# Another start for stationary weight parts, and sums of weight blocks at other steps

## The chip, the cores and the metric

The kernel runs on one core of one Trainium2 chip. Its metric is the device time of one execution in microseconds (us), the median of the runs.

## The reference

One hybrid layer over 256 tokens of width 1024, batch 1, all in float32:

```
h = rmsnorm(x) * (1 + scale) + shift          # shift, scale, gate = c @ w_ada + b_ada
qa ka va za qm km vm zm om ig fg ga gm = split(h @ w_in)     # w_in: 1024 x 11272
ya = (causal attention(qa, ka, va; 8 heads) * silu(za)) @ w_att_proj
hm = chunkwise mLSTM(silu(conv(qm, km)), vm, gates ig, fg; 4 heads)
ym = (rmsnorm(sigmoid(om) * hm) * silu(zm)) @ w_ml_proj
out = x + gate * ((sigmoid(ga) * ya + sigmoid(gm) * ym) @ w_out)
```

## The kernel before

**Products from split parts.** Each float32 operand of a large product is split into a rounded high part and the rest: h into hTh and hTl, a weight tile into wh (ScalarE, a copy, L502) and wl (VectorE, or GpSimd, named POOL, for some tiles, L506). A product is then three: high by high, low by high, high by low.

**Two orientations.** A chunk of 512 output columns is made in four groups, each with a pair of 128-row blocks of the contraction. Chunks of kind "tok" (va, zm, vm, out) have tokens on the output's partitions: the activation is stationary (128x128, loaded into the array), and the weight part streams (L1152 to L1154; for out L1145, and L1172 to L1174 at the end). Chunks of kind "ws" (za, qm, km, att, ga, gm, ml) are made transposed: a 128x128 piece of wh or wl is stationary, and 256 columns of an activation stream (L1159, L1161, L1162): hTh and hTl in za, qm, km, ga and gm, yah and yal in att, ymh and yml in ml. A group has 24 such products. The chunk om is made by seven products of half size, from sums of blocks (L1135 to L1137).

**Buffers.** wh and wl lie in two rings of five buffers of RING floats. WS_AT says how many floats into its buffer a part of a "ws" chunk begins; a part of another chunk begins at its start. Groups are numbered g in the order of place; split(g + 4) is issued at step g, four groups ahead of its products. Weight tiles (raw, six buffers of 1 MB) are loaded by the queue of SyncE (SP) as tiles come free. The output's activations yh and yl begin 16 and 48 floats into their slots (L851).

**Order.** Everything is issued in the order of the program, with no scheduler. Steps beside the main products are hooked to a step number g by at(g, function), and run there, in the order in which they were added, before the products of g. The gates' chain is such a row of steps: gates_0 to gates_5 work on the tile G on ScalarE, VectorE and POOL, gates_4 clears GE on POOL (L611), gates_5 writes GE (L619) and sends G's row to DRAM, gates_T transposes GE on TensorE (L641), gates_6 and gates_7 fetch and mask NM, gates_D takes its exponential.

**The sums.** Four sums of blocks of w_in (two halves each, om_sums in DRAM) are formed by DMAs that POOL issues: om_sum copies a block there (L770) or has a DMA add a block to it (L768). OM_SUMS lists them as (sum, source, add); a whole number as source is another sum. They are read as weight tiles for om later on.

Of the kernel before, what the change touches and what calls it, by code (L numbers as in the profile page):

```python
# [21 lines left out]
NEG = -1e30  # L22
BUCKETS = 32

RING, WS_AT = 1152, 96

COL = dict(qa=0, ka=1024, va=2048, za=3072, qm=4096, km=5120, vm=6144, zm=7168, om=8192,
           ig=9216, fg=9220, ga=9224, gm=10248)
# [21 lines left out]
NV = 344  # L50
OM_PRODUCTS = (((0, 0), 0), (1, 1), ((1, 0), 0), (2, 1), (0, 2), (3, 3), ((1, 1), 2))
OM_FIRST = (0, 1, 4, 5)
OM_SUMS = ((0, (0, 0), False), (2, (0, 1), False), (0, (0, 1), True), (2, (1, 1), True),
           (1, 0, False), (1, (1, 1), True), (3, 1, False), (3, (1, 0), True))
OM_SUM_AT = (5, 8, 11, 14, 20, 26, 32, 38)
W_PIECES = ((0, 512), (512, NR), (512, 1024), (1024, NR))


# [13 lines left out]
def tile_hybrid(ctx: ExitStack, tc: tile.TileContext, x, c, params2, w_row, w_va, ada_mod, ada_gate,  # L72
# [62 lines left out]
    adat, wrow, wsp, hf = {}, {}, {}, {}  # L135
# [235 lines left out]
    def start(name, half=0):  # L371
        return G0[C[name, half]]
# [138 lines left out]
    def at(step, fn, *a):  # L511
        hooks.setdefault(step, []).append((fn, a))
# [528 lines left out]
    at(start("gm") + 1, gate_read)  # L1041
    for q in range(4):
        at(start("ml") + 3 + q, gate_columns, q)
    for (i, src, add), step in zip(OM_SUMS, OM_SUM_AT):
        for hf in range(2):
            at(step + 3 * hf, om_sum, i, src, add, hf)
    T["A"] = {}
    for kh in range(2):
        at(start("qm", 1) + 1 + 4 * kh, h_full, kh)
# [179 lines left out]
```

## Time and profile before

| | |
|---|---|
| three runs | 355.93, 356.88, 356.96 us; median 356.88 |
| the profiled execution | 356.49 us, of which the span from the first to the last instruction is 354.6 |
| granted TensorE clock | 1.000 |
| DMA | 89.33 MB, mean 252 GB/s |
| the sums' queue (software_dynamic) | 8.39 MB, 10.3% of 16 engines' span |

PE is TensorE's products, PEld its weight loads, DVE VectorE, ACT ScalarE, POOL GpSimd, SP SyncE. Rows of groups give line, engine, operation, output<-inputs, shapes and count. "[1.10 <-ACT GE L619]" means that the engine was idle for 1.10 us before this, and what ended that. Starts of products are in us from the span's start; durations include the array's latency, so that products overlap: the pace is seen in the starts.

### The profile page before, as it was taken

Reading aid. Unit: us, or ns where it says so; the run is one execution under the profiler, and the core shown is the slowest. Engines: PE = TensorE matmul, PEld = TensorE weight load, DVE = VectorE, ACT = ScalarE, POOL = GpSimd, SP = SyncE. Lnnn points to the kernel's source line nnn. Section 1 sums busy time; section 2 is a strip of 40 time slices with the busy share of each in tenths; the row PEclk is TensorE's granted clock in tenths of the full one; section 3 lists DMA queues with packets and bytes.
Section 4 is the critical chain, followed back from the end, with each engine's and each line's share of the span. In section 5 each row is a group of like instructions: output and inputs, shape, how many; then the busy total and the mean of one; then the engine's idle time right before and its main releaser. Section 6 shows DMA issues by size and latency. Waiting matters only on the chain.

```text
span 354.6 us, 6241 instructions
## 1 busy us (share of the span) xinstructions
PE 348.4 (98%) x2420; PEld 327.1 (92%) x2420; DVE 262.8 (74%) x393; ACT 221.8 (63%) x344; POOL 100.9 (28%) x97
## 2 busy tenths in 40 slices
PE   8999999999999999999999999999999999999995
PEld 7787889999989999999998888888989999999995
DVE  5999987967973779865868665777777466689842
ACT  4868889799757857675636565677573463655410
POOL 4700004954501665665206242000002121302000
PEclk9999999999999999999999999999999999999999
DMA  7999999997997699395997916677999027363011
GB/s 303 417 415 414 416 418 405 262 365 208 240 298 242 211 357 344 103 352 203 262 355 239 368 81 224 214 273 266 150 262 387 6 86 299 151 206 152 2 61 59
DMA packets 29069, 89.33 MB, mean 252 GB/s; under 512 B 3368, under 2 KB 5296, under 8 KB 28336
## 3 DMA queue, kind: packets, MB, share of 16 engines
q1 hardware_dynamic: 26008, 80.02, 62.4%
q0 software_dynamic: 2880, 8.39, 10.3%
q10 hardware_dynamic: 152, 0.53, 0.4%
q8 instruction: 19, 0.31, 0.3%
q14 instruction: 10, 0.08, 0.1%
HBM read 87.68 MB, written 9.64 MB: 274 GB/s over the span
## 4 chain that ended last, share of the span: by engine, by line
PE 87%; DMA 4%; ACT 4%; DVE 3%; issue 0%; SPq 0%; ACTq 0%
PE mm L1162 13%; PE mm L1161 13%; PE mm L1159 13%; PE pm L203 12%; PE mm L1152 5%; PE mm L1153 5%; PE mm L1154 5%; PE mm L1145 3%; DMA raw<-in_w_in_dram 3%; PE aux L1135 2%; PE aux L1136 2%; PE aux L1137 2%; DVE wl L506 1%; DMA xt<-in_x_dram 1%; ACT wh L502 1%; PE xps L268 1%
## 5 line engine op out<-in xcount | busy, mean ns | idle before, releaser
L506 DVE TENSOR_TENSOR wl<-raw,wh 128x1024 fp32r<-128x1024 f32 (+1 forms) x98 | 121.2, 1253 | 55.1 <-ACT wh L502 54.4
L502 ACT CAST wh<-raw 128x1024 fp32r<-128x1024 f32 (+1 forms) x106 | 106.2, 1015 | 42.9 <-PE mm L1154 16.7
L1159 PE MATMUL mm<-hTh,wh 128*128 128x256 f32 x320 | 91.4, 286 | 0.0
L1162 PE MATMUL mm<-hTh,wl 128*128 128x256 f32 x320 | 90.2, 282 | 0.0
L1161 PE MATMUL mm<-hTl,wh 128*128 128x256 f32 x320 | 90.1, 282 | 0.0
L1159 PEld LDWEIGHTS mm<-hTh,wh 128*128 128x128 f32 x320 | 60.3, 189 | 0.2
L1161 PEld LDWEIGHTS mm<-hTl,wh 128*128 128x128 f32 x320 | 60.3, 188 | 0.2
L1162 PEld LDWEIGHTS mm<-hTh,wl 128*128 128x128 f32 x320 | 60.3, 188 | 0.0
L1152 PE MATMUL mm<-wh,hTh 128*128 128x512 f32 (+1 forms) x112 | 40.5, 362 | 0.0
L1153 PE MATMUL mm<-wl,hTh 128*128 128x512 f32 (+1 forms) x112 | 40.2, 359 | 0.0
L1154 PE MATMUL mm<-wh,hTl 128*128 128x512 f32 (+1 forms) x112 | 40.1, 358 | 0.0
L506 POOL TENSOR_TENSOR wl<-raw,wh 128x1024 fp32r<-128x1024 f32 x8 | 20.9, 2620 | 14.1 <-ACT wh L502 14.1
L1154 PEld LDWEIGHTS mm<-wh,hTl 128*128 128x128 f32 x112 | 21.0, 188 | 2.5
L1152 PEld LDWEIGHTS mm<-wh,hTh 128*128 128x128 f32 x112 | 21.0, 188 | 2.4
L1153 PEld LDWEIGHTS mm<-wl,hTh 128*128 128x128 f32 x112 | 21.1, 188 | 2.3
L188 ACT CAST wrh<-raw 128x512 fp32r<-128x512 f32 (+1 forms) x24 | 18.2, 762 | 7.4 <-DMA raw<-in_w_row_dram 7.4
L193 DVE TENSOR_TENSOR wrl<-raw,wrh 128x512 fp32r<-128x512 f32 (+1 forms) x26 | 20.5, 813 | 0.9 <-ACT wrh L188 0.9
L203 PE MATMUL pm<-wrh,hTh 128*128 128x512 f32 x64 | 19.9, 392 | 0.0
L203 PE MATMUL pm<-wrh,hTl 128*128 128x512 f32 x64 | 19.8, 390 | 0.0
L842 POOL TENSOR_TENSOR attT<-attT,gat 128x1024 f32<-128x1024 f32 x2 | 5.2, 2625 | 50.9 <-ACT gat L841 50.9
L203 PE MATMUL pm<-wrl,hTh 128*128 128x512 f32 x64 | 19.1, 395 | 0.0
L1162 PE MATMUL mm<-yah,wl 128*128 128x256 f32 x64 | 18.0, 281 | 0.0
(244 smaller groups left out, 753.2 us busy)
## 6 DMA issues: line engine op xcount, KB each, us to landing
raw<-in_w_in_dram SPq DMA_DIRECT2D x31, 1024.0 KB, 7.8
adat<-in_ada_mod_dram SPq DMA_DIRECT2D x16, 512.0 KB, 8.8
om_sum<-in_w_in_dram POOLq DMA_DIRECT2D x12, 512.0 KB, 9.6
raw<-in_w_va_dram SPq DMA_DIRECT2D x6, 688.0 KB, 8.9
raw<-in_ada_gate_dram SPq DMA_DIRECT2D x4, 1024.0 KB, 8.2
raw<-in_w_att_proj_dram SPq DMA_DIRECT2D x4, 1024.0 KB, 4.8
raw<-om_sum SPq DMA_DIRECT2D x8, 512.0 KB, 5.6
raw<-in_w_ml_proj_dram SPq DMA_DIRECT2D x4, 1024.0 KB, 5.8
```

The lines of the kernel that those rows point to most:

```text
L188: copy(wsp[k][0][:, c0:c1], wrow[k][:, c0:c1])
L193: e.tensor_tensor(l[:, cs], wrow[k][:, cs], h[:, cs].bitcast(F32), op=OP.subtract)
L203: nc.tensor.matmul(pm[ch][:, t], a[:, k, t * 128:(t + 1) * 128], b[:, cs], start=k == 0 and i == 0, stop=k == KT - 1 and i == 2)
L502: nc.scalar.copy(h, w)
L506: e.tensor_tensor(l, w, h.bitcast(F32), op=OP.subtract)
L1145: nc.tensor.matmul(mmt[ci][:, t, cs], a, w[:, kk, cs], start=first and i == 0 and c0 == 0 and w is wh, stop=last and i == 1 and c0 > 0, sk ...
L1152: nc.tensor.matmul(o, a, wh[:, kk], start=first, stop=False)
L1153: nc.tensor.matmul(o, a, wl[:, kk], start=False, stop=False)
L1154: nc.tensor.matmul(o, b, wh[:, kk], start=False, stop=last)
L1159: nc.tensor.matmul(o, wh[:, kk, cs], sh_[:, k], start=first and i % 2 == 0, stop=False, skip_group_check=True)
L1161: nc.tensor.matmul(o, wh[:, kk, cs], sl_[:, k], start=False, stop=False, skip_group_check=True)
L1162: nc.tensor.matmul(o, wl[:, kk, cs], sh_[:, k], start=False, stop=last and i % 2 == 1, skip_group_check=True)
```

## The change

It moves the start of stationary weight parts in their ring buffers from 96 to 80 floats (384 to 320 bytes). And it gives each sum its own step, with the second half two steps behind the first instead of three, in a slightly other order: the four adds to sums 0 and 2, which stood at steps 11 to 17, now stand at 18, 20, 26 and 28, behind the gates' steps 12 to 17.

```diff
-RING, WS_AT = 1152, 96
+RING, WS_AT = 1152, 80
...
-OM_SUMS = ((0, (0, 0), False), (2, (0, 1), False), (0, (0, 1), True), (2, (1, 1), True),
-           (1, 0, False), (1, (1, 1), True), (3, 1, False), (3, (1, 0), True))
-OM_SUM_AT = (5, 8, 11, 14, 20, 26, 32, 38)
+OM_SUMS = (((0, (0, 0), False), 5), ((2, (0, 1), False), 9), ((0, (0, 1), True), 18), ((1, 0, False), 24),
+           ((2, (1, 1), True), 26), ((1, (1, 1), True), 30), ((3, 1, False), 37), ((3, (1, 0), True), 41))
...
-    for (i, src, add), step in zip(OM_SUMS, OM_SUM_AT):
+    for (i, src, add), step in OM_SUMS:
         for hf in range(2):
-            at(step + 3 * hf, om_sum, i, src, add, hf)
+            at(step + 2 * hf, om_sum, i, src, add, hf)
```

## The prediction

> **What bounds the kernel now.** I read the page from the top: busy times, the clock row, the chain that ended last.
>
> ```profile
> PE 348.4 (98%) x2420; PEld 327.1 (92%) x2420; DVE 262.8 (74%) x393; ACT 221.8 (63%) x344; POOL 100.9 (28%) x97
> PEclk9999999999999999999999999999999999999999
> PE 87%; DMA 4%; ACT 4%; DVE 3%; issue 0%; SPq 0%; ACTq 0%
> ```
>
> TensorE runs 348.4 of 354.6 us at full granted clock and carries 87% of the chain. The time can only fall in two ways: TensorE's products follow each other faster, or its few idle moments go. The change has one part for each. For the pace I asked for the lines that multiply with a stationary weight part (L1159; L1161 and L1162 have the same counts) and for the tail of the output product (L1172), where the roles are exchanged: there the weights stream and yh is stationary.
>
> ```profile
> L1159 PEld LDWEIGHTS mm<-hTh,wh x320: 187/188/193, 82.9 to 305.8; 128*128 128x128 f32 x160
> L1159 PE MATMUL mm<-hTh,wh x320: 279/281/367, 83.0 to 305.9; 128*128 128x256 f32 x160
> L1159 PE MATMUL mm<-yah,wh x64: 279/281/285, 164.2 to 186.6; 128*128 128x256 f32 x64
> L1159 PE MATMUL mm<-ymh,wh x64: 279/281/285, 306.3 to 328.7; 128*128 128x256 f32 x64
> L1172 PEld LDWEIGHTS mm<-wh,yh x32: 187/188/188, 339.9 to 350.4; 128*128 128x128 f32 x32
> L1172 PE MATMUL mm<-wh,yh x32: 276/276/276, 340.0 to 350.5; 128*128 128x256 f32 x32
> ```
>
> Columns are minimum, median and maximum in ns. Both kinds stream 256 columns against a 128x128 stationary block of the same type, and the weight load takes 188 ns in both. Yet the product takes 276 ns without exception at L1172, and 279 to 285 with a stationary weight part. The busy table by stretch gives the pace (a window of length W that overlaps n products of length d has a pace of (W+d)/n):
>
> ```profile
> core 0: us, PE busy (x) PEld busy (x) DVE busy (x) ACT busy (x) POOL busy (x), PEclk, DMA share, GB/s
> 130.00:186.00 56.00, 56.00 (x474) 56.00 (x473) 43.54 (x71) 34.39 (x46) 26.51 (x16) 1.00 0.81 269
> 286.00:290.00 4.00, 4.00 (x36) 4.00 (x36) 1.97 (x4) 3.30 (x12) 1.25 (x1) 1.00 0.00 0
> 308.00:328.60 20.60, 20.60 (x176) 20.60 (x175) 17.58 (x18) 11.36 (x13) 4.58 (x3) 1.00 0.43 154
> 330.00:339.60 9.60, 9.60 (x87) 9.60 (x86) 7.77 (x9) 5.25 (x6) 0.00 (x0) 1.00 0.01 2
> 341.00:350.00 9.00, 9.00 (x82) 9.00 (x81) 3.92 (x8) 0.00 (x0) 0.00 (x0) 1.00 0.24 89
> ```
>
> The first three rows hold products with a stationary weight part: 56.281/474 = 118.7 ns, 4.281/36 = 118.9, 20.881/176 = 118.6. The last two hold the output product: 9.876/87 = 113.5 and 9.276/82 = 113.1. It is not other traffic: 118.9 stands in a row with no DMA at all, 118.7 in one at 269 GB/s. What differs is where the operands lie. In the built program hTh and hTl start 256 bytes past a multiple of 512; yah, yal, ymh, yml and the rings of wh and wl at a multiple of 512; yh 64 and yl 192 bytes past one. With every inner step a multiple of 512, the distance from the streamed to the stationary operand, modulo 512, is 128 for hTh and hTl and 384 for the four others (118.7 ns both), and 64 or 192 in the output product (113.3 ns).
>
> The second part concerns the one place where TensorE waits in mid-kernel:
>
> ```profile
> 105.31 0.27 PE L685 MATMUL aux<-ident,P 128*128 128x128 f32 x1
> 106.68 0.31 PE L641 MATMUL aux<-ident,GE 36*128 36x36 f32 x2 [1.10 <-ACT GE L619]
> ...
> 103.29 1.05 ACT L502 CAST wh<-raw 128x1024 fp32r<-128x1024 f32 x1 [2.12 <-DMA raw<-in_w_in_dram]
> 104.37 1.23 DVE L506 TENSOR_TENSOR wl<-raw,wh 128x1024 fp32r<-128x1024 f32 x1 [1.29 <-ACT wh L502]
> 105.71 0.41 DVE L618 TENSOR_TENSOR G<-G 4x256 f32<-4x256 f32 x1
> 106.21 0.41 ACT L619 ACTIVATE GE<-G 4x256 f32<-4x256 f32 x1 [0.62 <-DVE st L676]
> ```
>
> The transposes of GE (L641) wait 1.10 us for ScalarE's GE, that for VectorE's L618, which stands behind a wl, that behind a cast, and the cast waited 2.12 us for a weight load.
>
> **The change part by part.** *Offset.* No instruction is added or removed; every wh and wl of kind "ws" moves 64 bytes down in the same buffers. The distances become 64 (hTh, hTl) and 320 (the rest). 320+64+64 products on each of three lines are 1344. Nothing in the trace shows a weight part at 320. Bounds: if the distance is what counts, 64 is that of yh, so 113.3, a gain of 5.4 ns x 1344 = 7.3 us; the other end is the slowest steady pace of such products in the trace, in the ga stage (24 from 243.44 to 246.32, 120.0 ns):
>
> ```profile
> 243.44 0.29 PE L1159 MATMUL mm<-hTh,wh 128*128 128x256 f32 x1
> 246.32 0.40 PE L1135 MATMUL aux<-wh,hsum 128*128 128x512 f32 x1
> ```
>
> That would lose 1.3 x 1344 = 1.7 us. I take the end at 113.3, since 960 of the 1344 get exactly yh's distance and the tail is steady there for 192 products. I deduct 0.5 us: some 22 stretches begin behind other products, and I let the first five of each keep the old pace (22 x 5 x 5 ns).
>
> The Trainium skill, page "TensorE: Matmul & The Clock Gate", section "Step-by-step: what each phase is for", says that TensorE reads SBUF through two independent ports, one for the streamed operand and one for weight loads, so that loading the next weights takes nothing from the running product. By that rule this part would bring nothing and the sum would be that of the second rival below. Its weight loads agree (188 ns in both kinds); its products do not (276 against 279 to 285), though no row here shows that the offset is the cause.
>
> *Sums.* Sixteen DMAs of POOL form sums of weight blocks in DRAM (L770 copies, L768 adds into the destination). Only POOL's order changes. At the gates (om_sum_565/566 are the halves of sum 0, 569/570 of sum 2), before:
>
> ```order
> L589 TENSOR_SCALAR G<-G 4x256
> L770 DMA om_sum_566<-in_w_in_dram 256x1x512
> L770 DMA om_sum_569<-in_w_in_dram 256x1x512
> L770 DMA om_sum_570<-in_w_in_dram 256x1x512
> L768 DMA om_sum_565<-in_w_in_dram 256x1x512
> L598 TENSOR_TENSOR G<-G 4x256
> L600 TENSOR_TENSOR G<-G 4x256
> L768 DMA om_sum_566<-in_w_in_dram 256x1x512
> L768 DMA om_sum_569<-in_w_in_dram 256x1x512
> L611 MEMSET GE 36x256
> L768 DMA om_sum_570<-in_w_in_dram 256x1x512
> L704 TENSOR_TENSOR yal<-yf,yah 128x512
> ```
>
> and after, on the same engine (line numbers are one lower):
>
> ```order
> L588 TENSOR_SCALAR G<-G 4x256
> L769 DMA om_sum_569<-in_w_in_dram 256x1x512
> L769 DMA om_sum_570<-in_w_in_dram 256x1x512
> L597 TENSOR_TENSOR G<-G 4x256
> L599 TENSOR_TENSOR G<-G 4x256
> L610 MEMSET GE 36x256
> L703 TENSOR_TENSOR yal<-yf,yah 128x512
> L767 DMA om_sum_565<-in_w_in_dram 256x1x512
> L631 COPY NM<-NM 128x4x128
> ```
>
> All four adds leave the gates' stretch; one copy moves ahead of G's clearing. POOL's own issue time was never in the way:
>
> ```profile
> 75.01 0.88 POOL L586 TENSOR_SCALAR G<-G 4x256 f32<-4x256 f32 x1 [3.72 <-ACT G L584]
> ...
> 91.31 1.71 POOL L768 DMA_DIRECT2D om_sum<-in_w_in_dram  x2
> 93.06 0.31 POOL L611 MEMSET GE<- 36x256 f32 x1
> 97.98 0.41 DVE L612 TENSOR_TENSOR GE<-G 4x256 f32<-4x256 f32 x1
> ```
>
> The copy that moves ahead issues within the 3.72 us that POOL then waits for ScalarE, and GE is cleared at 93.4 and first written at 97.98. What the adds hold up is the DMA engines. Queues from 87 to 92.4 us, then from 92.4 to 103.3, then the page's median landing of all such loads:
>
> ```profile
> q0 software_dynamic: 256, 0.50, 69.5%
> ...
> q0 software_dynamic: 570, 1.11, 59.5%
> raw<-in_w_in_dram SPq DMA_DIRECT2D x3, 1024.0 KB, 14.2
> ...
> raw<-in_w_in_dram SPq DMA_DIRECT2D x31, 1024.0 KB, 7.8
> ```
>
> POOL's queue took 60 to 70% of the engines' time while weight loads took 14.2 us instead of 7.8. The load behind the late cast was issued at 92.47:
>
> ```profile
> 92.47 10.74 DMA raw<-in_w_in_dram
> ```
>
> At 7.8 us it lands at 100.3, before ScalarE is free for the cast (103.29-2.12 = 101.17). Then VectorE's 1.29 us go and GE comes 1.29 us earlier. TensorE, with 144 faster products behind it (0.8 us), would still be there first, so wait and products together give 1.3 us here; without the faster pace it is the 1.1 us of the wait. Next late is VectorE itself, which has no gap left there.
>
> The adds run later, between weight parts of POOL. Before (567/568 are the halves of sum 1):
>
> ```order
> L506 TENSOR_TENSOR wl<-raw,wh 128x1024
> L770 DMA om_sum_568<-om_sum_566 16x8192
> L506 TENSOR_TENSOR wl<-raw,wh 128x1024
> L768 DMA om_sum_567<-in_w_in_dram 256x1x512
> L506 TENSOR_TENSOR wl<-raw,wh 128x1024 x2
> L768 DMA om_sum_568<-in_w_in_dram 256x1x512
> ```
>
> and after:
>
> ```order
> L505 TENSOR_TENSOR wl<-raw,wh 128x1024 x2
> L769 DMA om_sum_567<-om_sum_565 16x8192
> L769 DMA om_sum_568<-om_sum_566 16x8192
> L767 DMA om_sum_569<-in_w_in_dram 256x1x512
> L505 TENSOR_TENSOR wl<-raw,wh 128x1024 x2
> L767 DMA om_sum_570<-in_w_in_dram 256x1x512
> L767 DMA om_sum_567<-in_w_in_dram 256x1x512
> ```
>
> Behind them on POOL wait wl parts, and TensorE for those. Loads that take 14.2 instead of 7.8 us delay a cast by up to 6.4 us; the split runs four steps ahead of the products (4 x 24 x 118.7 ns = 11.4 us), which covers that. I cost it at nothing; uncovered, an add would cost a microsecond or two. No gates' chain lies there.
>
> *Sum.* The profiled execution took 356.49 us. (1344-144) x 5.4 ns = 6.5, less 0.5, plus 1.3 is 7.3: 349.2. The median of the runs, 356.88, stands 0.4 higher, so 349.6.
>
> **Rivals.** *Part of the products only.* Distance 320 appears nowhere before; if yah, yal, ymh and yml keep 118.7, 384 x 5.4 = 2.1 us are missing: 351.7. Also, the pace has a memory. The va products at the same distance ran 12.716/83 = 153.2 ns each before the first transposes, and 157.8 behind them (23 in 3.63 us):
>
> ```profile
> 55.30:67.70 12.40, 12.40 (x83) 12.40 (x82) 11.13 (x13) 10.29 (x15) 8.91 (x7) 1.00 0.97 299
> 71.94 0.32 PE L1153 MATMUL mm<-wl,hTh 128*128 128x344 f32 x1
> 75.57 0.38 PE L658 MATMUL aux<-kT,qT 128*128 128x256 f32 x1
> ```
>
> If stretches behind transposes stay slow, it ends nearer 355.
>
> *No change of pace.* The distance may not be the cause: at L902 to L904, where SD lies 192 bytes from what streams, nine products take 1.08 us, 120 ns each.
>
> ```profile
> 268.94 0.28 PE L902 MATMUL aux<-vaug,SD 128*128 128x258 f32 x1
> 270.02 0.28 PE L1159 MATMUL mm<-hTh,wh 128*128 128x256 f32 x1
> ```
>
> Against it: two thirds of these stream 258 columns, and nine may be too few to settle. Then only the wait goes: 356.88-1.1 = 355.8.
>
> *Slower.* Distance 64 or 320 makes a worse rhythm in L1159 to L1162. It decides from (1.1+1.07)/1344 = 1.6 ns more per product, 120.3. At 120.0 the time is 357.5; with another 5.4 ns per product it is 363.1. Against it: 64 is good wherever the trace has it.
>
> **How the numbers follow.** Faster pace everywhere 0.42 (349.6, own range 348 to 351); part of the products 0.24 (351 to 355.3); no change of pace 0.18 (355.8); slower pace 0.16, of which 0.05 ends within 0.3%. That bound, 0.3% or 1.07 us, is about what runs of this kernel can tell from no change. 355.8 lies on it, so half of that case counts as faster: faster 0.42+0.24+0.09 = 0.75, same 0.09+0.05 = 0.14, slower 0.11. The low end lets all 1344 products count beside the wait (7.3+1.1 off the median is 348.5), less 0.6 for the spread of runs: 347.9. The high end is the unchanged pace plus 1 us for runs and moved adds: 356.8.
>
> **What would show it.** Right: products of L1158 to L1161 (one line lower) at 276 ns, 56 us holding some 496 instead of 474; no wait before the transposes of GE, loads between 87 and 103 us landing in about 8 us. The pace step is wrong if these products still take 279 to 285 ns, and half right if only those with hTh and hTl change. The cover of the moved adds is wrong if TensorE shows a wait for wl between 112 and 170 us.

## The result, and the profile after

| | before | after |
|---|---|---|
| median of the runs, same chip | 356.54 us (355.77 to 356.96, 5 runs) | 350.71 us (349.49 to 351.49, 5 runs) |
| ratio, 95% interval | | 0.9833 (0.9805 to 0.9861) |
| the profiled execution | 356.49 us, span 354.6 | 350.71 us, span 348.8 |

The change takes off 5.8 us, in the medians and in the spans alike. The forecast of 349.6 us was 1.1 us too low, inside its range and its likeliest case's own range (348 to 351). The first line is the page's busy times after; the second is the whole list of what TensorE waited for (us in total, times, longest):

```profile
PE 343.7 (99%) x2420; PEld 322.4 (92%) x2420; DVE 263.8 (76%) x393; ACT 221.3 (63%) x344; POOL 100.2 (29%) x97
```
```profile
PE warm L231 <- POOL ident masks.py:199: 1.4, 1, 1.4
```

TensorE is busy for 4.7 us less (348.4 before) and idle for 1.1 us less (354.6-348.4 = 6.2 before, 5.1 now). Both parts of the forecast are there: faster products and one wait less. The one wait left in the list is at the very start.

**The pace.** The lines with a stationary weight part (one line lower than before) and the output product, minimum, median and maximum in ns:

```profile
L1158 PE MATMUL mm<-hTh,wh x320: 276/276/369, 83.0 to 300.3; 128*128 128x256 f32 x160
L1158 PE MATMUL mm<-yah,wh x64: 276/276/277, 160.5 to 181.9; 128*128 128x256 f32 x64
L1158 PE MATMUL mm<-ymh,wh x64: 281/281/282, 300.6 to 322.9; 128*128 128x256 f32 x64
...
L1171 PE MATMUL mm<-wh,yh x32: 276/276/276, 334.2 to 344.7; 128*128 128x256 f32 x32
```

Before, the first three read 279/281. Now hTh (in the median) and yah have the 276 of the output product, and ymh has not: 281, and never under it. Yet yah and ymh start at the same place modulo 512 and lie at the same distance, 320, from their weight part. By a stretch I mean products of this kind that follow each other on TensorE with nothing else between, and with the same pair of parts streaming (hTh and hTl, yah and yal, or ymh and yml). The busy table shows the pace of the same groups (PE busy and count first; the first row lies within qm and km and att, the second within ml):

```profile
130.00:182.00 52.00, 52.00 (x462) 52.00 (x460) 42.67 (x69) 32.45 (x43) 27.32 (x18) 1.00 0.95 301
...
304.00:322.00 18.00, 18.00 (x155) 18.00 (x155) 16.15 (x18) 11.27 (x13) 3.30 (x2) 1.00 0.48 176
```

52.276/462 = 113.2 ns and 18.281/155 = 117.9 ns. Start by start, and past the first few products of a stretch, the trace has just two conditions. In one each product starts 113.3 ns behind the last; in the other the steps run 4 to 6 ns above that in turn, 117.8 in the mean. I call the first settled and the second unsettled. A stretch behind transposes or other products is settled from its first few products on, or never. Fifteen stretches begin with one step of 200 to 207 ns, in both kernels; these steps are left out here and below. Summed over all the other starts of the 1344 products, 7.4 us above 113.3 ns each before have become 2.4 us: 1.55 with hTh and hTl (288 of 960 products stand in unsettled stretches), 0.00 with yah and yal, 0.85 with ymh and yml. So the pace gives 5.0 us.

**The gates.** The same place on TensorE, ScalarE and VectorE as in the prediction:

```profile
104.87 0.27 PE L684 MATMUL aux<-ident,P 128*128 128x128 f32 x1
105.07 0.31 PE L640 MATMUL aux<-ident,GE 36*128 36x36 f32 x2
...
101.00 1.05 ACT L501 CAST wh<-raw 128x1024 fp32r<-128x1024 f32 x1
104.50 0.42 ACT L618 ACTIVATE GE<-G 4x256 f32<-4x256 f32 x1 [0.88 <-DVE st L675]
...
102.66 1.22 DVE L505 TENSOR_TENSOR wl<-raw,wh 128x1024 fp32r<-128x1024 f32 x1
```

No wait stands before the transposes of GE (1.10 us before), none before the cast (2.12) and none before the wl (1.29). GE still comes last there, but hardly: its weight load waits 0.17 us for it, and GE is done at 104.9 us (106.6 before). From the first transpose of P in this place (L682) to the next product with a weight part, TensorE took 1.98 us (104.66 to 106.64) where it took 3.16 before: 1.2 us. The queues hold no row of POOL's queue from 87 to 92.4 us (69.5% before), nor from 92.4 to 103.3 us (59.5%). The weight loads issued in the first stretch of time and in the second:

```profile
raw<-in_w_in_dram SPq DMA_DIRECT2D x2, 1024.0 KB, 4.9
...
raw<-in_w_in_dram SPq DMA_DIRECT2D x3, 1024.0 KB, 5.0
```

Before, the three of the second took 14.2 us in the median, the one behind the late cast 10.74. The two kernels of the next section that change one half each agree: in the same stretch of time loads took 13.4 us with the sums at their old steps and 5.4 with the new. One new loss stands against these gains, in the transposes of omt ahead of ml:

```profile
291.05 0.91 PE L938 MATMUL aux<-ident,omt 128*128 128x128 f32 x4
...
294.54 0.60 PE L938 MATMUL aux<-ident,omt 128*128 128x128 f32 x4
```

The four of the upper row take 0.3 us longer than those of the lower, since TensorE now comes there before VectorE has written omt: a weight load of L938 waits 0.3 us for L927, and none did before. 5.0+1.2-0.3 is 5.9, against 5.8 in the spans.

### The profile page after: what moved, and what is told of

Same layout as the page of the kernel before. It is cut to its first block, busy times and chain, and to the rows that moved or that the text cites. A ratio compares the mean times of both kernels' runs of the same rounds, so it can differ in the third digit from the quotient of the medians.

```text
span 348.8 us, 6239 instructions
## 1 busy us (share of the span) xinstructions
PE 343.7 (99%) x2420; PEld 322.4 (92%) x2420; DVE 263.8 (76%) x393; ACT 221.3 (63%) x344; POOL 100.2 (29%) x97
## 5 line engine op out<-in xcount | busy, mean ns | idle before, releaser
L505 DVE TENSOR_TENSOR wl<-raw,wh 128x1024 fp32r<-128x1024 f32 (+1 forms) x98 | 125.1, 1294 | 51.8 <-ACT wh L501 51.6
L1158 PE MATMUL mm<-hTh,wh 128*128 128x256 f32 x320 | 90.2, 282 | 0.0
L1161 PE MATMUL mm<-hTh,wl 128*128 128x256 f32 x320 | 88.9, 278 | 0.0
L1160 PE MATMUL mm<-hTl,wh 128*128 128x256 f32 x320 | 88.9, 278 | 0.0
L1158 PE MATMUL mm<-ymh,wh 128*128 128x256 f32 x64 | 18.0, 281 | 0.0
```

What stands on the lines that cost most here:

```text
L505: e.tensor_tensor(l, w, h.bitcast(F32), op=OP.subtract)
L1158: nc.tensor.matmul(o, wh[:, kk, cs], sh_[:, k], start=first and i % 2 == 0, stop=False, skip_group_check=True)
L1160: nc.tensor.matmul(o, wh[:, kk, cs], sl_[:, k], start=False, stop=False, skip_group_check=True)
L1161: nc.tensor.matmul(o, wl[:, kk, cs], sh_[:, k], start=False, stop=last and i % 2 == 1, skip_group_check=True)
```

## The experiments

The paces below are of stretches in which each product streams 256 columns. "Distance" is the start of the stationary operand less that of the streamed one, in bytes. "Settled" counts those of the 1344 products that lie in stretches whose mean pace, without the first step, is under 114.8 ns, from the starts in the one profiled execution of each kernel.

### Each half of the change alone

*offset_only*, against the kernel before:

```diff
-RING, WS_AT = 1152, 96
+RING, WS_AT = 1152, 80
```

> Only the start of the stationary weight parts moves (320 bytes), the sums stay at their old steps. Theory (the pace comes from the offset, the gates' wait from the sums): products with a stationary weight part keep the mixed pace of the changed kernel, 113.3 ns where a stretch settles and 117.8 where not, and the transposes of GE wait again about 1 us, so about 351.5 to 352 us. Rival (the moved DMAs set the pace): products at 118.7 ns, about 356.5 us.

Measured: 352.41 us (350.65 to 353.06), ratio 0.9876 (0.9853 to 0.9899), a little over what I expected. Stretch in qm and km, and the gates:

```profile
125.00:159.00 34.00, 34.00 (x303) 34.00 (x302) 30.29 (x46) 22.84 (x32) 21.60 (x12) 1.00 0.85 279
```
```profile
106.78 0.31 PE L641 MATMUL aux<-ident,GE 36*128 36x36 f32 x2 [1.39 <-ACT GE L619]
```

*sums_only*, against the changed kernel:

```diff
-RING, WS_AT = 1152, 80
+RING, WS_AT = 1152, 96
```

> Only the sums move; the weight parts stay at 384 bytes. Theory: products at 118.7 ns everywhere, the wait before the transposes of GE is gone, 355.3 to 355.8 us. Rival (the moved DMAs set the pace): about 351 us.

Measured: 355.31 us (355.14 to 356.09), ratio 0.9969 (0.9956 to 0.9983).

```profile
125.00:159.00 34.00, 34.00 (x289) 34.00 (x288) 28.28 (x46) 22.41 (x31) 22.75 (x14) 1.00 0.92 302
```
```profile
105.37 0.27 PE L684 MATMUL aux<-ident,P 128*128 128x128 f32 x1
105.57 0.31 PE L640 MATMUL aux<-ident,GE 36*128 36x36 f32 x2
```

The pace follows the offset alone: 34.276/303 = 113.1 ns with it, 34.281/289 = 118.6 without. The wait follows the sums alone: 1.39 us with the old steps (a little more than 1.10, since faster products bring TensorE there sooner), none with the new. Against 356.48 us of the same job the halves give 4.1 and 1.2 us, together 5.2, close to the 5.8 of both.

### Which distances settle

Six kernels move the weight parts, or h. *start_448*, *start_256*, *start_192*, *start_288* and *start_64* are the changed kernel with one number changed:

```diff
-RING, WS_AT = 1152, 80
+RING, WS_AT = 1152, 112      # start_448; 64, 48, 72 and 16 in the others
```

*h_moved* is start_256 with hTh and hTl, and the small prm2 and rvec ahead of them, 64 bytes lower, and all behind them where it was:

```diff
-    consts.tile([128, NPRM - 8], F32, name="free_prm")
+    consts.tile([128, NPRM - 24], F32, name="free_prm")
...
     hTl = consts.tile([128, KT, S], F32R, name="hTl")
+    consts.tile([128, 16], F32, name="pad_h")
```

> As the changed kernel, but weight parts start 448 bytes into their buffers: distance 192 to hTh and hTl, 448 to yah, yal, ymh, yml. Theory (an odd multiple of 64 bytes between stationary and streamed operand lets a stretch settle at 113.3 ns): settled and unsettled stretches as with 320, 349 to 352 us. Rival (320 is a good place of its own, or only a distance of 64 settles): products at 118 to 120 ns, about 355.5 us.

> As the changed kernel, but weight parts start 256 bytes into their buffers: distance 0 to hTh and hTl, 256 to the others. Theory (odd multiples of 64 settle, even ones don't): products with hTh and hTl at 118 to 120 ns, 355 to 357 us. Rival (any change away from 384 helps): about 351 us.

> The kernel with the weight parts 256 bytes in (start_256, 356.85 us, 120.0 ns per product everywhere), with hTh and hTl moved 64 bytes down (to 192 modulo 512, and with them the small tiles prm2 and rvec ahead of them). The weight parts stay where they are. Theory (the distance between the two operands counts): for hTh and hTl the distance is now 64, so their 960 products run at 117.8 or 113.3 ns by stretches, and the 384 with yah, yal, ymh, yml, still 256 apart, stay at 120.0; that takes off 960 x 2.2 = 2.1 us to 960 x 6.7 = 6.4 us: 350.5 to 354.7 us. Rival (the weight part's own address counts): all 1344 products stay at 120.0 and the time at 356.9 us, but for what the products of va, zm, vm and the moving of h's other readers change.

> Weight parts 192 bytes into their buffers: distance 448 for hTh and hTl and 192 for the others, both odd multiples of 64. Theory (an odd multiple of 64 bytes has two paces, 117.8 and 113.3 ns, and which of them a stretch takes depends on how it begins): no product at 118.7 or 120.0, a mixture of the two paces, 350 to 353 us. Rival (distances 64 and 320 are better than the others for a reason of their own): 118.7 ns or slower, 355.5 us or more.

> Weight parts 288 bytes into their buffers: distance 32 for hTh and hTl and 288 for the others, half of the step so far. If the two operands' places count in whole 64 bytes, 32 behaves like 0 or like 64, so a steady 120.0 ns (356.9 us) or a mixture of 117.8 and 113.3 ns (350 to 353 us); if they count more finely, a pace that no kernel here has shown yet.

> Weight parts 64 bytes into their buffers: distance 320 for hTh and hTl, 64 for yah, yal, ymh and yml. Theory (odd multiples of 64 bytes: 117.8 or 113.3 ns by stretch, by how a stretch begins): a mixture, 350 to 353 us, no product at 118.7 or 120.0. Rival (what settled so many stretches in the changed kernel is that hTh and hTl lie ahead of the weight part by just 64): hardly any stretch behind transposes settles, as with 192 and 448, and 352.5 to 353.5 us.

Rows of the busy table for the stretch in qm and km (with hTh and hTl), in this order: start_256, start_448, start_288, then h_moved with a second row, for att (with yah and yal):

```profile
125.00:159.00 34.00, 34.00 (x286) 34.00 (x285) 27.75 (x44) 21.98 (x31) 23.15 (x14) 1.00 0.92 303
```
```profile
125.00:159.00 34.00, 34.00 (x291) 34.00 (x291) 28.79 (x46) 22.39 (x31) 23.20 (x14) 1.00 0.92 305
```
```profile
125.00:159.00 34.00, 34.00 (x290) 34.00 (x289) 28.41 (x47) 22.39 (x31) 22.74 (x13) 1.00 0.91 303
```
```profile
125.00:159.00 34.00, 34.00 (x302) 34.00 (x302) 30.58 (x50) 22.45 (x32) 22.73 (x13) 1.00 0.94 308
165.00:181.00 16.00, 16.00 (x135) 16.00 (x135) 14.14 (x21) 8.12 (x10) 3.46 (x5) 1.00 0.96 318
```

That is 119.9, 117.8, 118.2, 113.5 and (16.28/135) 120.6 ns; in the last, short row one product more or less is worth 0.9 ns. By the starts, with times and ratios against the kernel before in the same job (medians of different jobs can't be compared to a few tenths):

| kernel | distance to hTh, hTl / the others | pace when not settled | settled of 1344 | median us | ratio (95%) |
|---|---|---|---|---|---|
| sums_only | 128 / 384 | 118.7 | 0 | 355.31 | 0.9969 (0.9956 to 0.9983) |
| offset_only | 64 / 320 | 117.8 | 840 | 352.41 | 0.9876 (0.9853 to 0.9899) |
| after | 64 / 320 | 117.8 | 864 | 350.71 | 0.9833 (0.9805 to 0.9861) |
| start_64 | 320 / 64 | 117.8 | 840 | 350.73 | 0.9823 (0.9787 to 0.9860) |
| start_448 | 192 / 448 | 117.8 | 336 | 352.89 | 0.9898 (0.9881 to 0.9914) |
| start_192 | 448 / 192 | 117.8 | 312 | 353.19 | 0.9896 (0.9873 to 0.9919) |
| start_288 | 32 / 288 | 118.3 | 0 | 354.73 | 0.9944 (0.9923 to 0.9965) |
| start_256 | 0 / 256 | 120.0 | 0 | 356.85 | 1.0018 (1.0007 to 1.0029) |
| h_moved | 64 / 256 | 117.8 / 120.0 | 600 / 0 | 353.35 | 0.9900 (0.9884 to 0.9917) |

h_moved tells distance from address: the weight parts lie where start_256 has them, and only the products whose other operand moved change, from 120.0 ns throughout to 600 of 960 settled, while those with yah, yal, ymh and yml stay at 120.0. Its gain over start_256 is 3.8 us in the spans of the profiled executions (355.0 and 351.2), less than the 4.4 us by which these products became shorter: the products in which hTh and hTl are stationary were moved as well, and those that stream 512 columns against them now start 228.9 ns apart, where they settled at 226.7 before (2.2 ns on 192 products). Their operands had been a multiple of 256 bytes apart, so the rule is of the 256-column products only.

The rows pair off. 64 and 320 behave alike, 192 and 448 alike, 128 and 384 alike, 0 and 256 alike: the distance counts modulo 256 bytes, not 512 as the prediction had it. At odd multiples of 64 a stretch can settle, readily at 64 and seldom at 192; at 128, 0 and 32 none did. start_448 missed its expected 349 to 352 us for that reason, and start_192 its 350 to 353, by 0.2: I had taken 64 and 192 as equal, since in the output product yh (64) and yl (192) both run at 113.3.

The second rival, no change of pace, had the support of the Trainium skill, page "TensorE: Matmul & The Clock Gate", section "Step-by-step: what each phase is for": two independent read ports, so that weight loads take no read bandwidth from the running product. Here the measurement decides: between sums_only and the changed kernel nothing but the start of the weight parts differs, and 1344 products take 5 us less. Why the distance counts, whether at the ports or elsewhere, no run shows.

### Is the pace taken over from the stretch ahead?

That would explain why ymh was unsettled and yah settled. Three kernels on the end of the program: *end_448* has gm and ml at 448, *ml_448* only ml, *gm_last_448* only gm's last 48 products, right ahead of ml; all else stays at 320.

```diff
-        at0 = WS_AT if chunks[place[g][0]]["kind"] == "ws" else 0
+        ch = chunks[place[g][0]]
+        at0 = 0 if ch["kind"] != "ws" else 112 if ch["name"] in ("gm", "ml") else WS_AT   # end_448
+        # ml_448:      112 if ch["name"] == "ml"
+        # gm_last_448: 112 if start("gm", 1) + 2 <= g < start("ml")
```

> The changed kernel, with the weight parts of the last two chunks pairs of kind ws (gm and ml) 448 bytes into their buffers and all others at 320. In the changed kernel the 192 products with ymh and yml ran at 117.8 ns, taken over from the stretch ahead of them; with all parts at 448 they ran at 113.3, again as the stretch ahead. Theory (a stretch that begins right behind another keeps its pace; the start in the buffer only decides how the stretches behind transposes settle): gm's last stretches and ml settle as they did with all at 448, 192 x 4.45 = 0.85 us and some 0.3 us of gm less, so 349.5 to 350 us; the yah products stay at 113.3. Rival (which pace is taken is chance): 350 to 351.5 us, and gm's last stretch may be unsettled again with ml behind it.

> The changed kernel with the weight parts of the chunk ml alone (the 192 products with ymh and yml) 448 bytes into their buffers; gm and all others stay at 320. Theory (a stretch right behind another keeps its pace): gm's last stretch is unsettled as in the changed kernel, so the products with ymh and yml stay at 117.8 ns although they ran at 113.3 from the same place in start_448 and end_448, and the time stays at that of the changed kernel, 350.5 us. Rival (448 suits these products better than 320): 113.3 ns, 0.85 us less, 349.7 us.

> The changed kernel with only the weight parts of gm's last two groups (48 products with hTh and hTl, the ones right ahead of ml) 448 bytes into their buffers; ml and all others stay at 320. In the three kernels that had these 48 products at a distance of 192 or 448 they ran at 113.3 ns, and ml behind them too. Theory (a stretch right behind another keeps its pace): these 48 products settle, and the 192 with ymh and yml, whose place is that of the changed kernel, where they ran at 117.8, now run at 113.3: 0.2 + 0.85 us less than the changed kernel of this job, a ratio of 0.997 between them. Rival (for ymh and yml the place decides): they stay at 117.8 and the two kernels differ by 0.2 us at most.

> The changed kernel once more, on the same chip as gm_last_448. Its time should be 350.5 us again, with the products with ymh and yml at 117.8 ns where gm's last group is unsettled, and at 113.3 where it is settled; in ml_448 gm's last group, unchanged there, had settled, so which of the two it is can differ between runs of one program.

Measured: end_448 349.65 us (349.32 to 350.68), ratio 0.9798 (0.9780 to 0.9817); ml_448 350.70 (349.62 to 351.71), 0.9830 (0.9792 to 0.9868); gm_last_448 349.89 (349.28 to 350.49), 0.9822 (0.9803 to 0.9841); after_again 350.78 (350.37 to 351.92), 0.9852 (0.9831 to 0.9872). The products with ymh of after_again, ml_448 and gm_last_448:

```profile
L1158 PE MATMUL mm<-ymh,wh x64: 276/276/276, 301.3 to 322.7; 128*128 128x256 f32 x64
```
```profile
L1159 PE MATMUL mm<-ymh,wh x64: 276/276/276, 300.7 to 322.1; 128*128 128x256 f32 x64
```
```profile
L1159 PE MATMUL mm<-ymh,wh x64: 276/276/280, 300.8 to 322.2; 128*128 128x256 f32 x64
```

And the stretch of ml in after_again, to be set beside the (x155) of the profile after:

```profile
304.00:322.00 18.00, 18.00 (x161) 18.00 (x160) 16.49 (x17) 11.27 (x13) 2.81 (x2) 1.00 0.48 176
```

after_again is the program of the changed kernel, and it shows ymh settled, at 18.276/161 = 113.5 ns. So neither the place of the operands nor the order of the program fixes the condition of a stretch. In it and in ml_448 gm's last 48 products were settled this time, and ml followed; ml_448 therefore could not test what it was made for. Wherever the start in the buffer does not change between two stretches that follow each other directly (hTh to yah, hTh to ymh; 16 cases in nine profiled executions at odd multiples of 64, throughout or up to there), the second had the condition of the first: 11 times settled, 5 times unsettled. The pace has a memory.

gm_last_448 shows its limit. Its 48 products stayed unsettled at 448, against my expectation, but behind them, with the start going from 448 to 320, ymh settled within three products (the 280 is of these; steps of 116, 123 and 118 ns, then 113). A change of distance can end the unsettled rhythm; in ml_448 the change from 320 to 448 left a settled one alone.

end_448 and gm_last_448 have the lowest times of all. I don't count either as shown to be faster than the changed kernel: gm_last_448 and after_again, on one chip, lie 0.9 us apart with runs that overlap (up to 350.49, from 350.37), and the profile of after_again has ymh settled too, so the mechanism that should make the difference is absent between the two profiles. Another difference is as large: the products of after_again take 1.05 us less in sum than those of the profile after (1104 settled against 864), but its span is only 0.2 us shorter, since its first product with a weight part starts 0.85 us later (83.86 against 83.01 us). In the other profiled executions that start lies between 82.77 (end_448) and 83.57 us, with waits of 0 to 1.4 us, mostly for ScalarE, ahead of it that the changes don't touch.

## Why the prediction was right, step by step

- **What bounds the kernel** (TensorE, by its pace and its few waits): right. The fall of 5.8 us is 4.7 of busy and 1.1 of idle time.
- **The distance sets the pace**: right in kind, shown by offset_only, sums_only and h_moved. The form was wrong in two ways: the period is 256 bytes, and a good distance permits the fast pace without ensuring it.
- **320 as good as 64**: right, by start_64 with both exchanged.
- **0.5 us for settling**: the mis-sized term. I let the first five products of each stretch keep the old pace; in fact a stretch settles or stays at 117.8 to its end, and the starts above 113.3 ns still cost 2.4 us (1.55+0.85) in the profiled execution. On the other side all 1344 products, those of the ga stage at 120.4 ns by their starts, had 7.4 us to give, where I counted 7.3. The forecast put the 144 products ahead of GE with the gates; counted in the same way, the other 1200 gave 4.5 us where I had 6.0, and this is the miss: the forecast fall of 7.3 us became 5.8. (The median of before, 356.54 beside the result and 356.88 when the forecast was made, makes the miss in the time itself 1.1.)
- **The gates, 1.3 us**: a little too small. That term held the wait and the 144 products ahead of it together, and in the traces the way from the first product with a weight part to the one behind the gates became 1.65 us shorter (25.28 before, 23.63 after): 1.2 at the place and 0.5 in the products. With the 4.5 of the others, less the 0.3 lost at omt, that makes the 5.8 to a tenth. sums_only, without the faster products, gave 1.2 in the medians. The mechanism (adds off the queues, load, cast, wl, GE) shows in each of its rows. GE came 1.7 us earlier, not 1.29; the load came even sooner than the 7.8 us I took from the median, in 5.0, with hardly anything but weight loads on the queues.
- **The moved adds at nothing**: right. TensorE shows no wait for wl in the whole program, and 125 to 159 us holds its products at 113.1 ns.
- **The transposes of omt**: not seen. TensorE, being earlier, now waits 0.3 us for VectorE there.
- **The rivals.** *Part of the products only* had the right mechanism, the pace's memory, but the wrong place: I feared for the products with yah and yal at 320, and they settled to the last, while 288 of the 960 with hTh and hTl, behind transposes and other products, did not, and ymh took over what stood ahead of it. *No change of pace* is excluded by offset_only. *Slower* was not this change, but its price is real: at a distance of 0 every product takes 120.0 ns, and start_256, with the gates' wait gone, is still 0.18% (0.07 to 0.29) slower than before.

What decides whether a stretch behind transposes settles stays open. The same stretch of the same program did and did not, with its first starts at the same spacing to within 10 ns. One sign is in the traces: at 64 or 320, of the stretches with hTh and hTl that begin with a step of 200 ns or more, all 32 whose first step took 205 to 207 ns settled, and 45 of the 83 at 200 to 204 (seven kernels, eight executions); at 192 or 448 it does not hold (0 of 5 and 5 of 30). So the first product's place in the rhythm has to do with it, as sign or as cause; one candidate, not tried, is the arrival of the products ahead, which at 291 us depends on a wait for VectorE and so differs from run to run.

## What to carry to other kernels

Where TensorE is the bound, compare the durations of products of one shape line by line: 279 to 281 against 276 ns looked like nothing and was worth 5 us over 1344 products here. Where they differ, look at where the two operands start relative to each other, and move one by 64 bytes at a time; it costs no instruction. Expect the gain by stretch, not by product: count the stretches that keep a slow rhythm before promising the whole.

## What the runs showed of the hardware that I had not expected

- For products of 256 columns the pace depends on the distance between the two operands modulo 256 bytes: 120.0 ns at 0, 118.3 at 32, 118.7 at 128, and 117.8 or 113.3 at 64 and 192.
- At the last two it has two conditions under the same program, operands and granted clock: ymh at 117.9 ns in one execution and at 113.5 in another (clock 1.000 and 0.999). A stretch handed its condition on to the one directly behind it in all 16 cases with the start unchanged.
- Beside POOL's copies and adds in DRAM weight loads took 14.2 us to land (13.4 in offset_only), in the same place without them 5.0 (5.4 in sums_only).
